# One S5 layer's response matrices: C loaded in another place, evicted in one piece, with the skip added by TensorE

## The chip, the core and the metric

The kernel runs on one core of a Trainium2 chip. The metric is the device time of one execution in microseconds, measured from outside; the profiler's span, from the first to the last instruction, stands beside it. Lower is better.

## The reference, cut to what matters

One inference step of a decoder trunk on 320 tokens (256 of a prompt, 8 samples of 8 tokens). The first layer is an S5 layer: 64 groups of 16 channels, each with 64 complex states, then a GLU. Behind it come a layer with latent attention, and after each of the two an attention to 256 memory tokens and an MLP. Only the S5 layer matters here:

```python
def s5_mixer(u, a_re, a_im, log_dt, b_re, b_im, c_re, c_im, d_skip, w_glu, h0_re, h0_im):
    ...
    _, _, h_re, h_im = lax.associative_scan(
        _complex_affine_combine, (a_seq_re, a_seq_im, bu_re, bu_im), axis=1)
    ...
    y = jnp.einsum('gkn,btgn->btgk', cr, h_re) - jnp.einsum('gkn,btgn->btgk', ci, h_im)
    y = y.reshape(bsz, t, dm) + d_skip.astype(f32) * u.astype(f32)
    g = jax.nn.gelu(y, approximate=False).astype(u.dtype)
    z = g @ w_glu
```

## The kernel before, in words

`s5_scan` computes the layer in chunks of 8 tokens (L = 8; 32 chunks of the prompt and 8 samples make 40 columns). The 64 groups are taken in four quarters `hq` of 16 groups, 8 from each half of the channels. For each quarter three matrices are made from the weights: `rt` turns a chunk's inputs into its state (`state_weights`, `state_turned`, `states`), `ca` turns the state before a chunk into its outputs (`out_weights`), and `tt` holds the responses of a chunk's outputs to its own inputs: a block Toeplitz matrix with 8x8 blocks of 16x16 for each group.

`responses(hq)` (L1097) has TensorE make the 8 blocks of one column, for 16 groups, in one PSUM bank `kps`: four rows of groups q on partitions 32q to 32q+15, four groups j side by side. For quarters 0 and 1, C's part comes in two matrices, `ca` and `ct`, so there are two matmuls for a group; for 2 and 3 one. `responses_out(hq)` (L1110) copies them to `kk` on 16 partitions with four activations (L1114), adds the skip weight D on the diagonal of the first block on GpSimd (`dd` at L1118, `kk` at L1119), and lets SP issue 8 transfers from `kk` to `tt`, one for each input position s (L1122): the first brings 8 blocks to 16 partitions of `tt`, the last one block. `kk` has one buffer, `tt` two. `outputs(hq, half)` (L1168) multiplies the inputs U by `tt` and the states HS by `ca` (and `ct`); its result is evicted (L1193), turned by TensorE and passed through the gelu (`outputs_turned`). `scan(f)` and `scanned(f)` bring the states of quarters 2f and 2f+1 from chunk to chunk; VectorE does the scan.

Between these stand sixteen `products(i)` (L736): matmuls that make the memory layer's keys and values, each of which also issues the weight load of `products(i + 4)` on SP (L219). Their results go out through a pair of buffers by `keys_out` and `values_out`: ScalarE copies, GpSimd issues the transfer (L765). `glu_load(0)` loads the first chunk of the GLU's weights, and `load_gains` nine small rows of gains (L413 to L416), both on SP.

The end of `s5_scan` is a written list of calls, and `in_order` (L600) ties all instructions of `s5_scan` on each engine to the order in which they are written. So an instruction that waits holds up its whole engine, and SP's transfers wait behind each other. Instructions of the GLU that follow can be put between them by the scheduler. SP's transfers take eight semaphores in turn; each waits for the one eight places earlier. `split_chunk` (L185) turns a loaded weight chunk into a high part on ScalarE (L193) and the rest on VectorE (L194) for the GLU's matmuls (L224 to L226).

Of the kernel before, what the change touches and what calls it, by code (L numbers as in the profile page):

```python
# [10 lines left out]
F32 = mybir.dt.float32  # L11
F32R = mybir.dt.float32r
I32 = mybir.dt.int32
AF = mybir.ActivationFunctionType
# [74 lines left out]
class Trunk:  # L89
# [577 lines left out]
    def s5_scan(self, sp, mkv, mn):  # L667
# [50 lines left out]
            PQ.dma_start(xc[i * NCH:i * NCH + NC_P], I['x_prompt'][0].rearrange("(c s) d -> c s d", s=L)[:, :, cols])  # L718
            PQ.dma_start(xc[i * NCH + NC_P:(i + 1) * NCH], I['x_sample'][:, :, cols])
        PQ.tensor_mul(dn, dn, gxn[:G])  # L720
        for i, part in enumerate(('re', 'im')):
            for o in range(2):
                PQ.dma_start(nat['c'][i * G:(i + 1) * G, :, o], I[f'ssm_c_{part}'][0])
        self.mem_load(0, mkv)
        load(0)
        for i, part in enumerate(('re', 'im')):
# [85 lines left out]
        T1 = pp.tile([128, 8, G], F32, name="T1")  # L812
        T2 = pp.tile([128, 8, G], F32, name="T2")
        sign = sp.tile([128, 1], F32, name="sign")
        U = sp.tile([128, G * NCH + 24], F32, name="U")
        tts = [sp.tile([128, L, 16, K], F32, name="tt", tag="tt", bufs=2) for _ in range(2)]
        V.memset(PR[:, 0], 1.0)
        V.memset(PI[:, 0], 0.0)
        V.memset(U[:, G * NCH:], 0.0)
        for hs, v in ((top, 1.0), (bot, -1.0)):  # L820
            V.memset(sign[hs], v)
        for t in tts:
# [45 lines left out]
        def power(m):  # L868
# [15 lines left out]
        cor, coi = w(8), w(9)  # L884
        power(2)

        V.tensor_mul(nat['b'][:, :, 0].rearrange("p k n -> p n k"),
                     bn.rearrange("p (n k) -> p n k", k=K), gxn[:, None, :].to_broadcast([2 * G, N, K]))
        power(4)


# [56 lines left out]
        p4 = lambda ap, gs: ap[:, :, gs].rearrange("p s g -> p g s")[:, :, :, None].to_broadcast([128, 8, L, K])  # L948
        b4 = lambda ap, gs: ap[:, gs, None, :].to_broadcast([128, 8, L, K])
        q4 = lambda ap, gs: ap[:, 1:9, gs].rearrange("p t g -> p g t")[:, :, :, None].to_broadcast([128, 8, L, K])  # L950
        bz = sp.tile([128, 64 * K], F32, name="bz")
        rbs, rts = {}, {}

        def state_weights(hq, hh):

            gs = slice(hh * 32 + 8 * hq, hh * 32 + 8 * hq + 8)
            rb = sp.tile([128, 8, L, K], F32, name="tq", tag="tmp4", bufs=2)
            t1 = sp.tile([128, 8, L, K], F32, name="tq", tag="tq")
            V.tensor_mul(rb, b4(BR, gs), p4(QX, gs))
            V.tensor_mul(t1, b4(BI, gs), p4(QY, gs))  # L960
            V.tensor_add(rb, rb, t1)
            rbs[hq, hh] = rb

        def state_turned(hq, hh):

            if hh == 0:
                rts[hq] = self.xp.tile([128, 2, 8, 128], F32, name="rt", tag="xl" if hq % 2 else "xh", padded_shape=[128, 2, 10, 128])
            rb, rt = rbs.pop((hq, hh)), rts[hq]
            b0 = (hq * 16 + hh * 8) * K
            A.activation(bz[:, b0:b0 + 8 * K].rearrange("p (g k) -> p g k", k=K), rb[:, :, L - 1], AF.Copy)  # L970
            for half in range(2):
                ps = tp("rps")
                for x in range(4):
                    self.transpose(ps[:, x * 128:(x + 1) * 128], rb[:, half * 4 + x].rearrange("p s k -> p (s k)"))
                A.activation(rt[:, hh, half * 4:half * 4 + 4], ps.rearrange("p (x c) -> p x c", x=4), AF.Copy)
# [61 lines left out]
        sc([128, 2, 8, 16])  # L1037
        HW = 32 * NCH
        HSs = [s8.tile([128, HW + 24], F32, name="HS")]
        dd = s8.tile([K, 2, 8, K], F32, name="dd")  # L1040
# [54 lines left out]
        kks = {}  # L1095

        def responses(hq):  # L1097

            ps = kks[hq] = at("kps")
            ca, ct = weights_of(hq)  # L1100
            for j in range(4):
                for q in range(4):
                    u = q * 4 + j
                    o = ps[q * 32:q * 32 + K, j * 128:(j + 1) * 128]
                    z = bz[:, (hq * 16 + u) * K:(hq * 16 + u + 1) * K]
                    nc.tensor.matmul(o, z, ca[u // 8][:, u % 8, 0:L, :], start=True, stop=ct is None, skip_group_check=True)
                    if ct is not None:
                        nc.tensor.matmul(o[:, K:], z, ct[u // 8][:, u % 8, 0:L - 1, :], start=False, stop=True, skip_group_check=True)

        def responses_out(hq):  # L1110
            ps = kks.pop(hq)
            kk = s8.tile([K, L, 16, K], F32, name="kk", tag="kk")
            for q in range(4):
                A.activation(kk[:, :, q * 4:(q + 1) * 4],  # L1114
                             ps[q * 32:q * 32 + K].rearrange("p (j t k) -> p t j k", j=4, t=L), AF.Copy)
            now = kk[:, 0].rearrange("p (h g) k -> p h g k", h=2)
            d = dT.rearrange("p (h g) -> p h g", h=2)[:, :, 8 * hq:8 * hq + 8, None]
            PQ.tensor_mul(dd, d.to_broadcast([K, 2, 8, K]), self.ident[:K, None, None, :K].to_broadcast([K, 2, 8, K]))  # L1118
            PQ.tensor_add(now, now, dd)  # L1119
            tt = tts[hq % 2]  # L1120
            for s in range(L):
                nc.sync.dma_start(tt[s * K:(s + 1) * K, s:], kk[:, 0:L - s])  # L1122


        def scan(f):
# [42 lines left out]
        def outputs(hq, half):  # L1168
            (ca, ct), tt, HS = weights_of(hq), tts[hq % 2], HSs[hq // 2]
            if half == 0:  # L1170
                if hq == 0:
                    ycs[0] = yc0.rearrange("p (s g k) -> p s g k", s=L, k=K)
                elif hq == 2:
                    ygs.append(sp.tile([128, 2, 1024], F32, name="yg", tag="cmat"))
                    ycs[2] = ygs[0][:, 0].rearrange("p (s g k) -> p s g k", s=L, k=K)
                else:
                    pool, tag = (s8, "ct0") if hq == 1 else (sp, "tmp4")
                    ycs[hq] = pool.tile([128, L, 8, K], F32, name="yc", tag=tag, bufs=2)
            ps = at("yps")
            for x in range(4):  # L1180
                gl = half * 4 + x
                n = 2 if ct is None else 3
                for st in range(n):
                    for hh in range(2):
                        g = hh * 32 + hq * 8 + gl
                        g2 = hh * 16 + hq % 2 * 8 + gl
                        o = ps[hh * 64:(hh + 1) * 64, x * 128:(x + 1) * 128]
                        if st == 0:
                            nc.tensor.matmul(o, U[:, g * NCH:g * NCH + 64], tt[:, :, hh * 8 + gl, :], start=True, stop=False)
# [84 lines left out]
        keys_turned(2)  # L1274
        responses(1)
        scanned(0)
        keys_out(2)
        outputs(0, 0)
        responses_out(1)
        outputs(0, 1)  # L1280
        state_weights(2, 0)
        state_turned(2, 0)
        keys_turned(3)
        state_weights(2, 1)
        state_turned(2, 1)
        keys_out(3)
        products(10)
        states(2)
        state_weights(3, 0)
        state_turned(3, 0)  # L1290
        products(11)
        values_out(5)
        state_weights(3, 1)
        state_turned(3, 1)
        states(3)
        outputs(1, 0)
        outputs(1, 1)
        outputs_turned(0)
        outputs_high(0)
        out_weights(2, 0)  # L1300
        out_weights(2, 1)
        products(12)
        responses(2)
        responses_out(2)
        outputs_turned(1)
        outputs_high(1)
        out_weights(3, 0)
        out_weights(3, 1)
        products(13)
        values_out(6)  # L1310
        glu = self.glu_load(0)
        responses(3)
        responses_out(3)
        scan(1)
        products(14)
        products(15)
        gn = self.load_gains(sp)
        scanned(1)
        outputs_low(0)
        outputs_low(1)  # L1320
# [1 line left out]
        outputs(2, 1)  # L1322
        final_states()
        self.chunks_ahead = [self.split_chunk(*glu)]
        values_out(7)
        outputs(3, 0)
        outputs_turned(2)
        outputs_high(2)
        outputs(3, 1)
        outputs_low(2)  # L1330
        outputs_turned(3)
        outputs_high(3)
        outputs_low(3)
# [748 lines left out]
```

## Time and profile before

| | us |
|---|---|
| median of 3 runs | 1212.83 |
| lowest, highest | 1210.83, 1215.29 |
| the profiled execution | 1214.25 |
| its span | 1212.6 |
| TensorE busy (share of the span) | 1130.1 (93%) |
| VectorE busy | 702.0 (58%) |
| ScalarE busy | 552.8 (46%) |
| GpSimd busy | 70.4 (6%) |

The busy times are of the profiled execution, and its own time is 1.42 us above the median of the runs. SP has no row: it computes nothing and only issues transfers. The shares are means over stages, so a stage has to be read by itself: the S5 layer takes about the first 160 us.

### The profile page before, as it was taken

Reading aid. Unit: us, or ns where it says so; the run is one execution under the profiler, and the core shown is the slowest. Engines: PE = TensorE matmul, PEld = TensorE weight load, DVE = VectorE, ACT = ScalarE, POOL = GpSimd, SP = SyncE. Lnnn points to the kernel's source line nnn. Section 1 sums busy time; section 2 is a strip of 40 time slices with the busy share of each in tenths; the row PEclk is TensorE's granted clock in tenths of the full one; section 3 lists DMA queues with packets and bytes.
Section 4 is the critical chain, followed back from the end, with each engine's and each line's share of the span. In section 5 each row is a group of like instructions: output and inputs, shape, how many; then the busy total and the mean of one; then the engine's idle time right before and its main releaser. Section 6 shows DMA issues by size and latency. Waiting matters only on the chain.

```text
span 1212.6 us, 21296 instructions
## 1 busy us (share of the span) xinstructions
PE 1130.1 (93%) x8233; PEld 1023.5 (84%) x8233; DVE 702.0 (58%) x1328; ACT 552.8 (46%) x1009; POOL 70.4 (6%) x118
## 2 busy tenths in 40 slices
PE   4899779899899999999999999999998999999997
PEld 3778669896599999999988985568965899999997
DVE  5898634575359643564587584426852675435643
ACT  3845354444345543453375353224443465434532
POOL 2101100000000000000000054200000000000001
PEclk8999989999899999999999999999999999999999
DMA  9243448746344454545462654547561434545441
GB/s 221 89 119 88 83 145 290 273 139 240 138 122 131 139 161 153 148 149 156 146 183 61 188 180 139 171 139 252 182 224 73 139 100 145 156 143 153 149 147 62
DMA packets 148657, 185.38 MB, mean 153 GB/s; under 512 B 15807, under 2 KB 116428, under 8 KB 148492
## 3 DMA queue, kind: packets, MB, share of 16 engines
q1 hardware_dynamic: 140812, 173.00, 46.6%
q0 software_dynamic: 4000, 7.91, 2.4%
q10 hardware_dynamic: 3744, 3.11, 0.8%
q8 instruction: 65, 1.06, 0.4%
q14 instruction: 36, 0.29, 0.1%
HBM read 175.41 MB, written 6.21 MB: 150 GB/s over the span
## 4 chain that ended last, share of the span: by engine, by line
PE 79%; ACT 7%; DMA 5%; issue 4%; DVE 2%; SPq 2%; POOL 0%; POOLq 0%; ACTq 0%; DVEq 0%
PE mm L224 19%; PE mm L225 19%; PE mm L226 19%; PE kt L102 2%; ACT whi L193 2%; PE sps L1458 2%; PE s L1941 2%; DMA wraw<-in_w_mem_q 2%; PE mm L750 1%; DMA wraw<-in_w_mem_k 1%; DMA wraw<-in_w_glu 1%; PE ops L1473 1%; PE pov L1515 1%; PE s L1982 1%; SPq L1122 1%
## 5 line engine op out<-in xcount | busy, mean ns | idle before, releaser
L194 DVE TENSOR_TENSOR wlo<-wraw,whi 128x1024 fp32r<-128x1024 f32 (+1 forms) x216 | 259.6, 1205 | 295.8 <-ACT whi L193 276.5
L193 ACT ACTIVATE whi<-wraw 128x1024 fp32r<-128x1024 f32 (+1 forms) x216 | 224.4, 1044 | 314.3 <-PE mm L225 249.1
L225 PE MATMUL mm<-xl,whi 128*128 128x320 f32 x944 | 294.4, 314 | 0.8 <-DVE xl L1704 0.6
L224 PE MATMUL mm<-xh,whi 128*128 128x320 f32 x944 | 281.5, 317 | 8.9 <-ACT xh L1485 4.5
L226 PE MATMUL mm<-xh,wlo 128*128 128x320 f32 x944 | 282.5, 312 | 0.0
L224 PEld LDWEIGHTS mm<-xh,whi 128*128 128x128 f32 x944 | 176.1, 191 | 11.8 <-ACT xh L1485 5.0
L225 PEld LDWEIGHTS mm<-xl,whi 128*128 128x128 f32 x944 | 180.6, 191 | 2.3 <-DVE xl L301 0.8
L226 PEld LDWEIGHTS mm<-xh,wlo 128*128 128x128 f32 x944 | 177.5, 191 | 0.0
L224 PE MATMUL mm<-hh,whi 128*128 128x320 f32 x512 | 158.0, 309 | 0.0
L225 PE MATMUL mm<-hl,whi 128*128 128x320 f32 x512 | 158.0, 309 | 0.0
L226 PE MATMUL mm<-hh,wlo 128*128 128x320 f32 x512 | 157.1, 308 | 0.0
L225 PEld LDWEIGHTS mm<-hl,whi 128*128 128x128 f32 x512 | 96.1, 188 | 0.0
L224 PEld LDWEIGHTS mm<-hh,whi 128*128 128x128 f32 x512 | 96.1, 188 | 0.0
L226 PEld LDWEIGHTS mm<-hh,wlo 128*128 128x128 f32 x512 | 95.9, 188 | 0.0
L102 PE MATMUL kt<-ident,kn 128*128 128x128 f32 x256 | 38.4, 285 | 7.3 <-ACT ktb L1385 4.2
L102 PEld LDWEIGHTS kt<-ident,kn 128*128 128x128 f32 x256 | 28.3, 143 | 19.5 <-ACT ktb L1385 6.8
L1870 POOL DMA_DIRECT2D rop<-in_cache_k_rope x64 | 34.4, 537 | 39.2 <-issue 16.6
L118 DVE TENSOR_TENSOR sq<-sq 128x320 f32<-128x320 f32 x67 | 32.3, 482 | 2.4 <-ACT sq L120 1.6
L1574 DVE TENSOR_TENSOR t_up<-t_up 128x320 f32<-128x320 f32 x64 | 29.8, 486 | 1.9 <-ACT hh L1573 1.8
L1575 DVE TENSOR_TENSOR hl<-t_up,hh 128x320 fp32r<-128x320 f32 x64 | 29.8, 487 | 0.9
L1383 DVE COPY ktb<-kt 128x512 f32<-128x512 f32 x32 | 22.0, 688 | 12.4 <-PE kt L102 11.9
L1573 ACT ACTIVATE hh<-t_up 128x320 fp32r<-128x320 f32 x64 | 28.4, 472 | 0.9
(493 smaller groups left out, 1805.1 us busy)
## 6 DMA issues: line engine op xcount, KB each, us to landing
wraw<-in_w_mlp_up SPq DMA_DIRECT2D x64, 512.0 KB, 3.7
wraw<-in_w_mlp_down SPq DMA_DIRECT2D x64, 512.0 KB, 3.5
kn<-in_cache_mem_k SPq DMA_DIRECT2D x16, 1024.0 KB, 7.1
vn<-in_cache_mem_v SPq DMA_DIRECT2D x16, 1024.0 KB, 9.7
wraw<-in_w_glu SPq DMA_DIRECT2D x32, 256.0 KB, 3.9
wraw<-in_w_mem_q SPq DMA_DIRECT2D x16, 512.0 KB, 6.8
wraw<-in_w_mem_o SPq DMA_DIRECT2D x16, 512.0 KB, 3.8
lat<-in_cache_kv_latent SPq DMA_DIRECT2D x64, 128.0 KB, 2.6
```

The costliest lines, as they stand in the source:

```text
L102: return self.nc.tensor.transpose(out, in_, self.ident[b:b + k, b:b + k])
L118: eng.tensor_add(st['acc'], st['acc'], st['last'])
L193: nc.scalar.activation(hi[:, :cols], raw[:, :cols], AF.Copy)
L194: nc.vector.tensor_sub(lo[:, :cols], raw[:, :cols], hi[:, :cols].bitcast(F32))
L224: nc.tensor.matmul(ps, wh, xh, start=start, stop=False)
L225: nc.tensor.matmul(ps, wh, xl, start=False, stop=False)
L226: nc.tensor.matmul(ps, wl, xh, start=False, stop=stop)
L1458: nc.tensor.matmul(sps[h * 32:(h + 1) * 32, :MT], qm[:, h * 2 + db, j * 128 + i * 32:j * 128 + (i + 1) * 32], ktb[:, h * 2 + db, :], start ...
L1573: A.activation(hh[b // 4][:, b % 4, :], a, AF.Square)
L1574: V.tensor_mul(a, a, a)
L1575: V.tensor_sub(hl[b // 4][:, b % 4, :], a, hh[b // 4][:, b % 4, :].bitcast(F32))
L1870: last[eng] = eng.dma_start(dst, src[bass.ds(v, 1)].rearrange("o p d -> (o p) d"))
```

## The change

It does four things. The four transfers of C are written further down, in a block that is to be issued after the VectorE operation `gained`. `responses` lets TensorE add the skip weights, by one more matmul of the identity with `dd` for each group, and makes its tiles 32 partitions high (16 of them from a neighbour's columns of `bz`, never read), so that all 128 partitions of the bank are written. `responses_out` evicts the bank with one activation into `kk` with 128 partitions and two halves, and issues four transfers for each s, one for each q. And in the list of calls `keys_out(2)`, `keys_out(3)`, `values_out(5)` and `values_out(7)` stand later, `products(12)` to `(14)`, `glu_load(0)` and `load_gains` earlier.

```diff
@@ s5_scan, loads @@
-        for i, part in enumerate(('re', 'im')):
-            for o in range(2):
-                PQ.dma_start(nat['c'][i * G:(i + 1) * G, :, o], I[f'ssm_c_{part}'][0])
...
+        gained = V.tensor_mul(nat['b'][:, :, 0].rearrange("p k n -> p n k"),
+                              bn.rearrange("p (n k) -> p n k", k=K), gxn[:, None, :].to_broadcast([2 * G, N, K]))
+        with tc.issue_after(gained.ins):
+            for i, part in enumerate(('re', 'im')):
+                for o in range(2):
+                    PQ.dma_start(nat['c'][i * G:(i + 1) * G, :, o], I[f'ssm_c_{part}'][0])
@@ responses @@
+            d = dT.rearrange("p (h g) -> p h g", h=2)[:, :, 8 * hq:8 * hq + 8, None]
+            PQ.tensor_mul(dd.rearrange("p (h g) k -> p h g k", h=2), d.to_broadcast([K, 2, 8, K]),
+                          self.ident[:K, None, None, :K].to_broadcast([K, 2, 8, K]))
...
-                    o = ps[q * 32:q * 32 + K, j * 128:(j + 1) * 128]
-                    z = bz[:, (hq * 16 + u) * K:(hq * 16 + u + 1) * K]
-                    nc.tensor.matmul(o, z, ca[u // 8][:, u % 8, 0:L, :], start=True, stop=ct is None, skip_group_check=True)
+                    o = ps[q * 32:(q + 1) * 32, j * 128:(j + 1) * 128]
+                    z = bz[:, hq, u * K:(u + 2) * K]
+                    nc.tensor.matmul(o, z, ca[u // 8][:, u % 8, 0:L, :], start=True, stop=False, skip_group_check=True)
...
+                    nc.tensor.matmul(o[:, :K], self.ident[:K, :2 * K], dd[:, u, :], start=False, stop=True, skip_group_check=True)
@@ responses_out @@
-            kk = s8.tile([K, L, 16, K], F32, name="kk", tag="kk")
-            for q in range(4):
-                A.activation(kk[:, :, q * 4:(q + 1) * 4],
-                             ps[q * 32:q * 32 + K].rearrange("p (j t k) -> p t j k", j=4, t=L), AF.Copy)
-            now = kk[:, 0].rearrange("p (h g) k -> p h g k", h=2)
...
-            PQ.tensor_add(now, now, dd)
+                kk_of.append(s8.tile([128, 2, L, 4, K], F32, name="kk", tag="kk", padded_shape=[128, 4, L, 4, K]))
+            kk = kk_of[0][:, hq % 2]
+            A.activation(kk, kks.pop(hq).rearrange("p (j t k) -> p t j k", j=4, t=L), AF.Copy)
             tt = tts[hq % 2]
             for s in range(L):
-                nc.sync.dma_start(tt[s * K:(s + 1) * K, s:], kk[:, 0:L - s])
+                for q in range(4):
+                    nc.sync.dma_start(tt[s * K:(s + 1) * K, q, s:], kk[q * 32:q * 32 + K, 0:L - s])
@@ the list of calls @@
         scanned(0)
-        keys_out(2)
         outputs(0, 0)
...
         state_turned(2, 0)
+        keys_out(2)
         keys_turned(3)
...
-        keys_out(3)
         products(10)
         states(2)
+        keys_out(3)
...
         states(3)
+        values_out(5)
+        products(12)
+        glu = self.glu_load(0)
         outputs(1, 0)
...
-        products(12)
+        products(13)
         responses(2)
...
-        products(13)
         values_out(6)
-        glu = self.glu_load(0)
+        products(14)
+        gn = self.load_gains(sp)
         responses(3)
         responses_out(3)
         scan(1)
-        products(14)
         products(15)
-        gn = self.load_gains(sp)
         scanned(1)
...
-        values_out(7)
         outputs(3, 0)
...
         outputs_low(2)
+        values_out(7)
         outputs_turned(3)
```

How this moves instructions is seen on three queues. First SP, from the responses of the last quarter to the GLU's weights; `tt<-kk` are the responses' transfers, `gn` the gains, `wraw` weights. Before:

```order
L1122 DMA tt<-kk 16x2048
L1122 DMA tt<-kk 16x1792
L1122 DMA tt<-kk 16x1536
L1122 DMA tt<-kk 16x1280
L1122 DMA tt<-kk 16x1024
L1122 DMA tt<-kk 16x768
L1122 DMA tt<-kk 16x512
L1122 DMA tt<-kk 16x256
L413 DMA gn<-in_norm_mix_pre 16x128
```

The same place after the change:

```order
L416 DMA gn<-in_q_norm 3x128
L1125 DMA tt<-kk 16x512 x4
L1125 DMA tt<-kk 16x448 x4
L1125 DMA tt<-kk 16x384 x4
L1125 DMA tt<-kk 16x320 x4
L1125 DMA tt<-kk 16x256 x4
L1125 DMA tt<-kk 16x192 x4
L1125 DMA tt<-kk 16x128 x4
L1125 DMA tt<-kk 16x64 x4
L182 DMA wraw<-in_w_glu 128x2x256 x6
```

Eight transfers became 32 with the same bytes, the gains stand ahead of them, and the first GLU weights but one chunk stay behind them. The other three quarters changed in the same way.

Second, ScalarE's queue from the states HS to the fourth quarter's outputs `yc`; `yg` are those of the third, `whi` the splits of GLU weights. Before:

```order
L1163 ACTIVATE HS<-H 64x16x32
L1193 ACTIVATE yg<-yps 128x8x64
L193 ACTIVATE whi<-wraw 128x1024
L1193 ACTIVATE yg<-yps 128x8x64
L193 ACTIVATE whi<-wraw 128x1024
L790 ACTIVATE wlo<-mm,r_mem 128x256 x2
```

And after:

```order
L1166 ACTIVATE HS<-H 64x16x32
L1196 ACTIVATE yg<-yps 128x8x64 x2
L193 ACTIVATE whi<-wraw 128x1024 x2
L1196 ACTIVATE yc<-yps 128x8x64
L1212 ACTIVATE yg<-ytp 128x80x4 x2
L193 ACTIVATE whi<-wraw 128x1024
```

The first split no longer stands between the two evictions of `yg`, and the last `values_out` (`wlo<-mm`) is gone from this place. Third, GpSimd's queue at the start, with its waits; `natc` is C, `dn` and `hn` are D and the states that come in. Before:

```order
L720 TENSOR_TENSOR dn<-dn,gxn 64x16 [waits DMASW2_49,DMASW0_49]
L723 DMA natc<-in_ssm_c_re 64x16x64
L723 DMA natc<-in_ssm_c_re 64x16x64 [waits DMASW1_49]
L723 DMA natc<-in_ssm_c_im 64x16x64
L723 DMA natc<-in_ssm_c_im 64x16x64 [waits DMASW3_49]
```

And after:

```order
L720 TENSOR_TENSOR dn<-dn,gxn 64x16 [waits DMASW2_49,DMASW0_49]
L891 DMA natc<-in_ssm_c_re 64x16x64
L891 DMA natc<-in_ssm_c_re 64x16x64 [waits DMASW1_49]
L891 DMA natc<-in_ssm_c_im 64x16x64
L891 DMA natc<-in_ssm_c_im 64x16x64 [waits DMASW3_49]
```

Only the line numbers differ; no wait on VectorE has come in.

## Rows read from the trace of the kernel before

**Rows 1.** The page: the span in 40 slices, TensorE's busy tenths and GB/s moved.

```profile
PE   4899779899899999999999999999998999999997
...
GB/s 221 89 119 88 83 145 290 273 139 240 138 122 131 139 161 153 148 149 156 146 183 61 188 180 139 171 139 252 182 224 73 139 100 145 156 143 153 149 147 62
```

**Rows 2.** SP's queue in order of time: start us, us, engine line op out<-in xcount.

```profile
75.88 7.26 SPq L1122 DMA_DIRECT2D tt<-kk  x8
...
138.76 5.96 SPq L1122 DMA_DIRECT2D tt<-kk  x8
```

**Rows 3.** The chain that ended last, where it runs through SP: start us, us, what.

```profile
138.76 0.51 SPq L1122
139.31 0.59 SPq L1122
139.95 0.59 SPq L1122
...
144.13 0.59 SPq L1122
...
145.24 0.35 SPq L413
...
148.45 0.23 SPq L415
...
149.08 0.39 SPq L182
```

**Rows 4.** ScalarE in order of time, with idle time before a row and its releaser.

```profile
72.61 2.40 ACT L1114 ACTIVATE kk<-kps 16x512 f32<-16x512 f32 x4 [2.03 <-PE kps L1108]
...
92.56 0.60 ACT L1193 ACTIVATE wlo<-yps 128x512 f32<-128x512 f32 x1
...
135.28 2.39 ACT L1114 ACTIVATE kk<-kps 16x512 f32<-16x512 f32 x4 [6.07 <-DMA tt<-kk]
...
154.74 1.06 ACT L193 ACTIVATE whi<-wraw 128x1024 fp32r<-128x1024 f32 x1 [11.27 <-DMA wraw<-in_w_glu]
```

**Rows 5.** TensorE in order of time, 59 to 163 us.

```profile
59.32 2.06 PE L1058 MATMUL sps<-U,rt 128*64 128x40 f32 x64
...
85.68 0.44 PE L1189 MATMUL yps<-tt,U 128*64 128x128 f32 x4
...
93.21 0.44 PE L1189 MATMUL yps<-tt,U 128*64 128x128 f32 x4 [3.20 <-ACT wlo L1193]
...
95.98 1.09 PE L102 MATMUL rps<-ident,tq 128*128 128x128 f32 x8
...
111.62 0.30 PE L1189 MATMUL yps<-tt,U 128*64 128x128 f32 x1
...
117.09 1.09 PE L102 MATMUL ytp<-ident,wlo 128*128 128x128 f32 x8
118.02 3.62 PE L752 MATMUL mm<-wraw,mnp 128*128 128x256 f32 x16
121.57 1.46 PE L1106 MATMUL kps<-hca,bz 128*16 128x128 f32 x32
122.96 1.09 PE L102 MATMUL ytp<-ident,yc 128*128 128x128 f32 x8
...
156.33 1.97 PE L102 MATMUL ytp<-ident,yg 128*128 128x128 f32 x8 [7.61 <-ACT yg L1193]
158.23 0.70 PE L1189 MATMUL yps<-tt,U 128*64 128x128 f32 x4
...
162.46 0.39 PE L224 MATMUL mm<-xh,whi 128*128 128x320 f32 x1
```

**Rows 6.** The transfers of line L1122: time from issue to landing.

```profile
DMA to landing us min/median/max: 2.2/4.0/5.1
```

**Rows 7.** Busy time in a stretch: engines, then granted TensorE clock, DMA share, GB/s.

```profile
156.00:158.00 2.00, 1.67 (x8) 1.57 (x8) 0.74 (x1) 2.00 (x5) 0.00 (x0) 0.50 0.00 0
```

**Rows 8.** The DMA view, 138 to 148 us: queue, packets, MB, share of 16 engines.

```profile
q1 hardware_dynamic: 382, 0.62, 55.3%
```

**Rows 9.** GpSimd in order of time.

```profile
6.28 1.67 POOL L723 DMA_DIRECT2D natc<-in_ssm_c_re  x2
```

More of the change, by code (lines that the diff above doesn't have):

```diff
@@ L814, in s5_scan @@
         sign = sp.tile([128, 1], F32, name="sign")
+        bz = sp.tile([128, 4, 17 * K], F32, name="bz")
         U = sp.tile([128, G * NCH + 24], F32, name="U")
-        tts = [sp.tile([128, L, 16, K], F32, name="tt", tag="tt", bufs=2) for _ in range(2)]
+        tts = [sp.tile([128, 4, L, 4, K], F32, name="tt", tag="tt", bufs=2) for _ in range(2)]
         V.memset(PR[:, 0], 1.0)
@@ L819, in s5_scan @@
         V.memset(U[:, G * NCH:], 0.0)
+        V.memset(bz[:, :, 16 * K:], 0.0)
         for hs, v in ((top, 1.0), (bot, -1.0)):
@@ L885, in s5_scan @@
         power(2)
-        V.tensor_mul(nat['b'][:, :, 0].rearrange("p k n -> p n k"),
-                     bn.rearrange("p (n k) -> p n k", k=K), gxn[:, None, :].to_broadcast([2 * G, N, K]))
+        gained = V.tensor_mul(nat['b'][:, :, 0].rearrange("p k n -> p n k"),
[4 more added lines that the diff above has]
+                    PQ.dma_start(nat['c'][i * G:(i + 1) * G, :, o], I[f'ssm_c_{part}'][0])
         power(4)
@@ L950, in s5_scan @@
         q4 = lambda ap, gs: ap[:, 1:9, gs].rearrange("p t g -> p g t")[:, :, :, None].to_broadcast([128, 8, L, K])
-        bz = sp.tile([128, 64 * K], F32, name="bz")
         rbs, rts = {}, {}
@@ L968, in state_turned @@
             rb, rt = rbs.pop((hq, hh)), rts[hq]
-            b0 = (hq * 16 + hh * 8) * K
-            A.activation(bz[:, b0:b0 + 8 * K].rearrange("p (g k) -> p g k", k=K), rb[:, :, L - 1], AF.Copy)
+            b0 = hh * 8 * K
+            A.activation(bz[:, hq, b0:b0 + 8 * K].rearrange("p (g k) -> p g k", k=K), rb[:, :, L - 1], AF.Copy)
             for half in range(2):
@@ L1039, in s5_scan @@
         HSs = [s8.tile([128, HW + 24], F32, name="HS")]
-        dd = s8.tile([K, 2, 8, K], F32, name="dd")
+        dd = s8.tile([K, 16, K], F32, name="dd")
         ca_of = lambda q: [s8.tile([128, 8, 9, K], F32, name="ca", tag=f"ca{q}", bufs=2) for _ in range(2)]
@@ L1093, in weights_of @@
             return ca, cts.get(hq)
-        kks = {}
+        kks, kk_of = {}, []
         def responses(hq):
+            d = dT.rearrange("p (h g) -> p h g", h=2)[:, :, 8 * hq:8 * hq + 8, None]
+            PQ.tensor_mul(dd.rearrange("p (h g) k -> p h g k", h=2), d.to_broadcast([K, 2, 8, K]),
+                          self.ident[:K, None, None, :K].to_broadcast([K, 2, 8, K]))
             ps = kks[hq] = at("kps")
@@ L1103, in responses @@
                     u = q * 4 + j
-                    o = ps[q * 32:q * 32 + K, j * 128:(j + 1) * 128]
-                    z = bz[:, (hq * 16 + u) * K:(hq * 16 + u + 1) * K]
-                    nc.tensor.matmul(o, z, ca[u // 8][:, u % 8, 0:L, :], start=True, stop=ct is None, skip_group_check=True)
+                    o = ps[q * 32:(q + 1) * 32, j * 128:(j + 1) * 128]
+                    z = bz[:, hq, u * K:(u + 2) * K]
+                    nc.tensor.matmul(o, z, ca[u // 8][:, u % 8, 0:L, :], start=True, stop=False, skip_group_check=True)
                     if ct is not None:
-                        nc.tensor.matmul(o[:, K:], z, ct[u // 8][:, u % 8, 0:L - 1, :], start=False, stop=True, skip_group_check=True)
+                        nc.tensor.matmul(o[:, K:], z, ct[u // 8][:, u % 8, 0:L - 1, :], start=False, stop=False, skip_group_check=True)
+                    nc.tensor.matmul(o[:, :K], self.ident[:K, :2 * K], dd[:, u, :], start=False, stop=True, skip_group_check=True)
         def responses_out(hq):
-            ps = kks.pop(hq)
-            kk = s8.tile([K, L, 16, K], F32, name="kk", tag="kk")
-            for q in range(4):
-                A.activation(kk[:, :, q * 4:(q + 1) * 4],
-                             ps[q * 32:q * 32 + K].rearrange("p (j t k) -> p t j k", j=4, t=L), AF.Copy)
-            now = kk[:, 0].rearrange("p (h g) k -> p h g k", h=2)
-            d = dT.rearrange("p (h g) -> p h g", h=2)[:, :, 8 * hq:8 * hq + 8, None]
-            PQ.tensor_mul(dd, d.to_broadcast([K, 2, 8, K]), self.ident[:K, None, None, :K].to_broadcast([K, 2, 8, K]))
-            PQ.tensor_add(now, now, dd)
+            if not kk_of:
+                kk_of.append(s8.tile([128, 2, L, 4, K], F32, name="kk", tag="kk", padded_shape=[128, 4, L, 4, K]))
+            kk = kk_of[0][:, hq % 2]
+            A.activation(kk, kks.pop(hq).rearrange("p (j t k) -> p t j k", j=4, t=L), AF.Copy)
             tt = tts[hq % 2]
             for s in range(L):
-                nc.sync.dma_start(tt[s * K:(s + 1) * K, s:], kk[:, 0:L - s])
+                for q in range(4):
+                    nc.sync.dma_start(tt[s * K:(s + 1) * K, q, s:], kk[q * 32:q * 32 + K, 0:L - s])
         def scan(f):
@@ L1188, in outputs @@
                         if st == 0:
-                            nc.tensor.matmul(o, U[:, g * NCH:g * NCH + 64], tt[:, :, hh * 8 + gl, :], start=True, stop=False)
+                            nc.tensor.matmul(o, U[:, g * NCH:g * NCH + 64], tt[:, (hh * 8 + gl) // 4, :, gl % 4, :], start=True, stop=False)
                         else:
@@ L1291, in s5_scan @@
         products(11)
-        values_out(5)
         state_weights(3, 1)
```

## The prediction

> **What bounds the kernel now.** Read the page's slices first [rows 1]. Each slice is 30.3 us. From the ninth on TensorE is busy nine tenths or more nearly everywhere, so there a later start is passed on whole. The slack lies in the first eight, where the S5 layer stands, and everything the change touches lies between 60 and 163 us. Then read the SP queue [rows 2]: `responses_out` issues eight transfers `tt<-kk` for each of four quarters, in 7.26 us the first time and 5.96 us the last. Then the chain of waits, which gives them one by one [rows 3], and last the two engines that wait on them, ScalarE [rows 4] and TensorE [rows 5]. Three stalls are plain in ScalarE's rows: the eviction into `kk` waits 6.07 us for the transfers before it, since there is one `kk`; and a weight split waits 11.27 us for a GLU weight that SP could issue only after the last responses and the gains. TensorE's first GLU matmul starts at 162.46 us. That instant is what I follow: the change is worth what it moves it by.
>
> **What the change takes away.** Four evictions of 16 partitions (2.40 us) become one on 128 partitions; the nearest row of that shape is 0.60 us [rows 4]. The GpSimd addition behind it goes off the path. `kk` gets two halves, so the 6.07 us wait goes; the split is now queued behind both evictions of `outputs(2)`, so the 11.27 us no longer stand before the second of them. I count all of these at nothing except the first: a later `tt` covers them, as the next parts show.
>
> **What it adds on TensorE.** 16 matmuls of 32x16 for each quarter, 32 records. The nearest small ones are `sps`, 64 records in 2.06 us [rows 5], so 32 take at most 1.0 us; the 32 records of `responses(2)` take 1.4 us with eight times the columns, which is no lower. I take 0.9 us, four times; nothing to 1.0 us are the ends.
>
> **What it adds on SP.** This decides. Each burst of 8 becomes 32 issues, with the same bytes. A large piece is slowed by the transfers ahead of it, but the unhindered issues of a burst show a price that hardly hangs on size: 0.59 us for 112 KB (the one at 139.31), 0.59 for 96 KB, 0.59 for 16 KB (the last), and 0.64 us from start to start [rows 3]. The new pieces are 32 KB to 4 KB. From other tensors come cheaper ones: the nine gain loads from HBM take 145.24 to 149.08, 0.43 us each, and the least, with two rows, 0.23 us. So the bounds are 0.43 and 0.65 us; I take 0.63, since the same tensors at nearly the same size show it. A burst then holds SP for 32 x 0.63 = 20.2 us, and its last piece lands 31 x 0.63 + 2.2 = 21.7 us after the first issue, with the least landing time [rows 6].
>
> **The sum, instant by instant.** `responses(0)` ends about when `kk` starts, 72.61 us. Plus 0.9 for the matmuls and 0.7 for the eviction and its hand-over, SP starts at 74.2 (75.88 before) [rows 2]. `tt` is whole at 74.2 + 21.7 = 95.9. TensorE, in order, stands at `outputs(0, 0)`, which started at 85.68. A half of `outputs(0)` takes 2.7 us (93.21 to 95.98, by the starts of it and the next work), and an eviction with hand-over 0.7 stands between: 95.9 + 2.7 + 0.7 + 2.7 = 102.0 against 95.98, so **6.0 us lost**; the 3.2 us that TensorE waited before that second half, which the later `keys_out(2)` removes, lie inside.
>
> Nothing shortens the run of TensorE to 111.62, so `outputs(1, 0)` would come at 117.6, and at 121.2 with `products(12)` moved ahead of it (3.55 us, 118.02 to 121.57). The second burst starts when `outputs(0, 0)` and `kk` are evicted, 98.6 + 1.4 = 100.0; SP, free of the first burst at 94.4 and of three weight loads behind it (0.5 each) at 96, is ready. Its `tt` is whole at 121.7, a half microsecond late. From there `outputs(1)` 5.5 us (111.62 to 117.09), the turn 0.9, `products(13)` 3.55, `responses(2)` 1.4 + 0.9, eviction 0.7: SP starts the third burst at 134.6.
>
> Now SP itself is the path. Third burst 20.2, to 154.8; then the nine gain loads, which the change moves ahead of the fourth burst, 3.84, to 158.6 [rows 3]; the fourth burst's `tt` is whole at 158.6 + 21.7 = 180.3. Its `kk` is ready long before, since `responses(3)` follows `responses(2)` within 7 us, and the scan, moved by the same 6.0 us, too. `outputs(3, 0)` waits for the transfers. TensorE has by then idled twice for over 10 us; after its idle time before 156 us the granted clock was 0.50 for two microseconds, so 1.2 GHz [rows 7], and the eight turns took 1.97 us where they take 1.09 at the full clock [rows 5]. So `outputs(3, 0)`, 16 matmuls where the 2.7 us held 24, takes 3.6 us, up to 3.9 with its start, the turn 1.9, and from `outputs(3, 1)` to the first GLU matmul it is 162.46 - 158.23 = 4.2: 180.3 + 3.9 + 1.9 + 4.2 = 190.3. That is **27.9 us later** than 162.46. Six GLU weight loads stand right behind the fourth burst (178.8), so they land by then. What comes after has the same order; the last `values_out` now stands after `outputs(3)` and the second weight split needs its buffer, which can cost some 3 us more, and prefetch can give that back.
>
> The profiled execution took 1214.25 us (span 1212.6), 1.4 above the median of the three runs, so 1214.25 + 27.9 - 1.4 = **1241 us**.
>
> Loading C later I count at nothing. The wait that the block adds holds only for instructions on VectorE, where `gained` runs; the transfers are GpSimd's, and the order shows them in the same place with no wait on VectorE.
>
> **The rivals.** *Cheap issues.* If a piece costs what a gain load does, 0.43 us, a burst holds SP for 13.8 us and `tt` is whole after 15.5. Then `outputs(0)` ends at 95.8, no loss; the third burst starts at 128.1, the gains end at 145.7, the last `tt` is whole at 161.2 and GLU starts at 171.2: 8.7 late, 1221.5 us. For it: all these are rows with 16 or fewer partitions from the same queue. Against it: the shortest of the 32 `tt` issues takes 0.51 us, the first of its burst, on an idle queue [rows 3].
>
> *Issues hidden behind transfers, so faster.* SP's rows may show long issues only because the transfers ahead of them are slow, and 32 small ones may pass as fast as their bytes allow. The window of the last burst has the hardware queue at 55.3% of 10 us, 5.5 us for 0.62 MB [rows 8]. With bursts of 6 us the third starts at 128, the gains end at 138, the last `tt` is whole at 146.3 and GLU starts at 153.5, now at the full clock, because none of the removed waits is replaced: 9 us early, 1204 us. It decides at about 0.33 us for a piece: with 7.2 us from the last `tt` to GLU, 162.46 - 128.1 - 3.84 - 2.2 - 7.2 = 21.1 us are left for 63 issues. Against it: the last piece of each burst, 16 KB, still takes 0.59 us with nothing ahead that it must wait for, and only transfers of two or three rows are under 0.33 [rows 3]. The Trainium skill, "DMA: Bandwidth & Descriptors", section "Issuing engines are not separate DMA queues", holds that the time on the sequencer to start a DMA is usually small relative to the DMA itself. By that rule the bursts would end as in this rival, at 1204 us; the row at 144.13 speaks against it, since 16 KB, a thirty-sixth of the burst's bytes, cost a tenth of the burst's issue time.
>
> *C does move.* Then 1.05 MB leave the start, where the first weights are waited for; at the 290 GB/s of the seventh slice [rows 1] that is 3.6 us at most, and the sum is 1237 to 1241. Against it: their place on their queue, where they start at 6.28 us now [rows 9], is the same in both orders.
>
> **How the numbers follow.** Forecast, issues of 0.55 to 0.70 us: 0.75, at 1233 to 1250 us with the 3 us behind GLU's start. Cheap issues, 0.35 to 0.55: 0.19, at 1217 to 1233. Hidden issues: 0.03. C moves, with the forecast's issues: 0.03. I take 1241. The range reaches down to the price of the gain loads and up to 0.70 us with the late split: 1221 to 1250. A measurement can tell about 0.5%, 6 us, from no change. Slower by more: all of the forecast and most of the cheap issues, 0.93; within: their lowest part, 0.04; faster: the hidden issues, 0.03.
>
> **What would show it.** In the profile after: 128 `tt<-kk` issues of about 0.58 us, bursts of some 20 us in SP's rows; TensorE idle before `outputs(0, 0)` until about 96, before `outputs(2, 0)` until about 156 and before `outputs(3, 0)` until about 180; the first GLU matmul near 190; the GpSimd rows of `natc` still at 6 to 9 us; no wait of `kk` on `tt`. It is wrong if the pieces take under 0.5 us, if `outputs(3, 0)` starts before 170 us, or if GLU starts late and the end does not.

## The result, and the profile after

The change makes the kernel slower, and by more than my range allowed. Five runs of each, side by side:

| | before | after |
|---|---|---|
| median, us | 1214.05 | 1264.46 |
| lowest, highest | 1210.83, 1216.19 | 1256.38, 1266.69 |
| ratio (95% interval) | | 1.0387 (1.0346 to 1.0428) |
| profiled execution, span | 1214.25, 1212.6 | 1256.38, 1254.7 |

I forecast 1241 us, between 1221 and 1250. The profiled execution of the changed kernel is the lowest of its five, 8.1 us under their median; the trace therefore accounts for 42.1 us of the 50.4 between the medians, and the rest stays without a row.

The slices of the page show idle time of TensorE where it was expected. Compare with [rows 1]:

```profile
PE   4999966999989999999998999999999999999997
```

Slices six and seven, 157 to 220 us, now hold idle TensorE; from the eighth on nothing has changed in kind. Slices three to five read busy and hide the rest of the loss, as the rows below show. SP's queue in order of time has the long bursts of the forecast, beside [rows 2]:

```profile
83.31 20.73 SPq L1125 DMA_DIRECT2D tt<-kk  x32
...
111.11 21.94 SPq L1125 DMA_DIRECT2D tt<-kk  x32
...
152.44 20.11 SPq L1125 DMA_DIRECT2D tt<-kk  x32
172.64 0.52 SPq L413 DMA_DIRECT2D gn<-in_norm_mix_pre  x1
...
174.60 1.57 SPq L413 DMA_DIRECT2D gn<-in_norm_mlp_pre  x1
...
177.72 20.13 SPq L1125 DMA_DIRECT2D tt<-kk  x32
```

The view of the tile `tt` gives the price of one piece, with its least, median and longest time in ns, and the time to landing, which answers to [rows 6]:

```profile
L1125 SPq DMA_DIRECT2D tt<-kk x128: 512/587/1609, 83.3 to 197.3; - x128
...
DMA to landing us min/median/max: 1.7/1.9/3.6
```

So far the forecast holds: 0.587 us for a piece, 20.1 to 21.9 us for a burst. But the first burst starts at 83.31 us where I had 74.2. ScalarE's rows, beside [rows 4], say what it waited for:

```profile
82.68 0.60 ACT L1121 ACTIVATE kk<-kps 128x512 f32<-128x512 f32 x1 [11.18 <-PE kps L1115]
...
151.81 0.60 ACT L1121 ACTIVATE kk<-kps 128x512 f32<-128x512 f32 x1 [7.69 <-PE kps L1115]
```

The eviction is one row of 0.60 us, as hoped, and no `kk` waits for `tt` any more; it waits 11.18 us for TensorE's matmuls of line L1115, the skip. TensorE in order of time, with idle time before a row in brackets, beside [rows 5]:

```profile
71.58 0.41 PE L1111 MATMUL kps<-ca,bz 128*32 128x128 f32 x2
71.82 0.36 PE L1113 MATMUL kps<-ct,bz 128*32 128x112 f32 x2
72.10 0.23 PE L1115 MATMUL kps<-dd,ident 16*32 16x16 f32 x2
72.27 0.41 PE L1111 MATMUL kps<-ca,bz 128*32 128x128 f32 x2
...
94.01 0.41 PE L1111 MATMUL kps<-ca,bz 128*32 128x128 f32 x2
...
96.63 0.23 PE L1115 MATMUL kps<-dd,ident 16*32 16x16 f32 x2 [2.03 <-POOL dd L1102]
...
107.11 0.44 PE L1192 MATMUL yps<-tt,U 128*64 128x128 f32 x4
...
133.94 0.29 PE L1192 MATMUL yps<-tt,U 128*64 128x128 f32 x1 [0.59 <-DMA tt<-kk]
...
143.77 0.41 PE L1111 MATMUL kps<-hca,bz 128*32 128x128 f32 x2
...
151.71 1.09 PE L102 MATMUL ytp<-ident,yc 128*128 128x128 f32 x8
...
197.21 0.66 PE L1192 MATMUL yps<-tt,U 128*64 128x128 f32 x2 [20.29 <-DMA tt<-kk]
198.43 0.47 PE L1192 MATMUL yps<-tt,U 128*64 128x128 f32 x1 [0.56 <-DMA tt<-kk]
...
202.83 0.44 PE L1192 MATMUL yps<-tt,U 128*64 128x128 f32 x4
...
207.68 1.40 PE L102 MATMUL ytp<-ident,yc 128*128 128x128 f32 x8 [2.89 <-ACT yc L1196]
...
208.95 0.62 PE L224 MATMUL mm<-xh,whi 128*128 128x320 f32 x1
```

From one group to the next it is 72.27 - 71.58 = 0.69 us, sixteen groups 11.0 us. In the kernel before the same stretch reads:

```profile
70.66 0.43 PE L1106 MATMUL kps<-ca,bz 128*16 128x128 f32 x8
...
71.08 0.42 PE L1106 MATMUL kps<-ca,bz 128*16 128x128 f32 x8
...
72.45 3.72 PE L750 MATMUL mm<-mnp,whi 128*128 128x256 f32 x16
```

Each matmul leaves two records, so x8 are four groups, one in each strip of 32 columns of the array, and they start together: four groups in 71.08 - 70.66 = 0.42 us, all sixteen in 72.45 - 70.66 = 1.8 us. In the changed kernel every row is one matmul (x2), and each starts 0.17 to 0.28 us after the one before. The idle bracket does not show this: the engine counts as busy, at the full granted clock (1.00 in the stretch from 71.5 to 82.6 us), while one strip works at a time.

GpSimd, beside [rows 9]: C starts where it did, and the diagonal blocks `dd` of the second quarter now stand on the path, behind two output transfers:

```profile
6.27 1.67 POOL L891 DMA_DIRECT2D natc<-in_ssm_c_re  x2
...
94.51 1.44 POOL L762 DMA_DIRECT2D out<-wlo  x2 [5.88 <-ACT wlo L787]
95.97 0.61 POOL L1102 TENSOR_TENSOR dd<-dT,ident 16x256 f32<-16x256 f32 x1
```

### The profile page after: what moved, and what is told of

It is laid out like the page before. It is cut to its first block, busy times and chain, and to the rows that moved or that the text cites. A ratio compares the mean times of both kernels' runs of the same rounds, so it can differ in the third digit from the quotient of the medians.

```text
span 1254.7 us, 21614 instructions
## 1 busy us (share of the span) xinstructions
PE 1163.6 (93%) x8361; PEld 1043.3 (83%) x8361; DVE 700.3 (56%) x1329; ACT 545.9 (44%) x997; POOL 68.1 (5%) x114
## 4 chain that ended last, share of the span: by engine, by line
PE 76%; SPq 5%; ACT 5%; issue 5%; DMA 4%; DVE 3%; POOL 0%; POOLq 0%; ACTq 0%; DVEq 0%
PE mm L225 18%; PE mm L224 18%; PE mm L226 18%; SPq L1125 4%; PE kt L102 2%; PE sps L1461 2%; PE s L1944 2%; DMA whi<-in_w_mem_k 2%; ACT whi L193 1%; DMA wraw<-in_w_glu 1%; PE ops L1476 1%; PE pov L1518 1%; PE s L1985 1%; DMA wraw<-in_w_mem_q 1%; PE ltp L102 1%
## 5 line engine op out<-in xcount | busy, mean ns | idle before, releaser
L1192 PE MATMUL yps<-tt,U 128*64 128x128 f32 x128 | 16.9, 295 | 22.1 <-DMA tt<-kk 21.4
L1192 PEld LDWEIGHTS yps<-tt,U 128*64 128x64 f32 x128 | 11.6, 148 | 24.1 <-issue 22.1
```

The costliest lines, as they stand in the source:

```text
L1192: nc.tensor.matmul(o, U[:, g * NCH:g * NCH + 64], tt[:, (hh * 8 + gl) // 4, :, gl % 4, :], start=True, stop=False)
```

## The experiments

| kernel | median, us | ratio (95% interval) | first GLU matmul, us |
|---|---|---|---|
| changed, skip behind | 1246.25 | 1.0238 (1.0198 to 1.0278) | 196.6 |
| changed, skip of 128 rows | 1243.58 | 1.0221 (1.0196 to 1.0247) | 194.4 |
| before, wide strips | 1216.05 | 1.0001 (0.9986 to 1.0016) | 168.0 |
| before, skip by TensorE alone | 1240.39 | 1.0195 (1.0170 to 1.0220) | 189.4 |
| before, list of the change | 1213.14 | 0.9981 (0.9965 to 0.9998) | 162.3 |
| before, list and mended skip | 1215.68 | 1.0004 (0.9985 to 1.0023) | 166.7 |
| before, C late in fact | 1212.12 | 0.9973 (0.9951 to 0.9994) | 163.9 |
| skip of 128 rows, two queues | 1219.20 | 1.0033 (1.0017 to 1.0048) | 170.4 |
| before, list and C late | 1209.02 | 0.9948 (0.9930 to 0.9965) | 162.1 |
| the same, splits held | 1202.51 | 0.9906 (0.9875 to 0.9938) | 151.0 |
| the change mended | 1212.10 | 0.9970 (0.9951 to 0.9989) | 157.1 |

Each ratio is to runs of the kernel before on the same chip (1214.9 to 1215.9 us); the last column is of each profiled execution, and between executions the S5 stage as a whole lies up to 4 us earlier or later. Two of the profiled executions lie apart from their medians: 1226.21 us with the wide strips, 1196.07 us with the splits held.

**The skip matmuls behind the others.** In `responses`, the changed kernel:

```diff
-                    nc.tensor.matmul(o[:, :K], self.ident[:K, :2 * K], dd[:, u, :], start=False, stop=True, ...)
+            for j in range(4):
+                for q in range(4):
+                    u = q * 4 + j
+                    o = ps[q * 32:(q + 1) * 32, j * 128:(j + 1) * 128]
+                    nc.tensor.matmul(o[:, :K], self.ident[:K, :2 * K], dd[:, u, :], start=False, stop=True, ...)
```

Issued behind the others, the skip isn't added to every group's sum, so this run is read for the time of its instructions, which are all there.

> The changed kernel with one edit: the sixteen skip matmuls of a quarter stand behind all its other matmuls instead of one behind each group. The trace of the changed kernel has the matmuls of the first quarter from 71.58 to 82.58 us, 11.0 us, 0.69 us for each group; before the change four groups, one in each strip of 32 columns, started within 40 ns of each other. Theory: the skip matmul, with 16 rows between matmuls of 128 rows, lets the groups no longer run side by side. Then this kernel needs 1.7 us as before plus 0.2 to 1.0 us for sixteen small ones, at most 2.7 us for a quarter; the rest of my first sum holds, the long bursts of SP decide, and the first GLU matmul starts near 190 us (208.95 in the changed kernel, 162.46 before): 19 us less, so about 1238 to 1246 us. The Trainium skill, page TensorEngine Tiling (Array Packing), section Key Properties, states that a change of the tiling mode drains the engine; with that rule this is the outcome. Rival: strips 32 columns wide, or a third matmul in a group, end the concurrency by themselves; then a quarter still takes some 8 to 11 us and the time stays near 1264.

TensorE's rows of the first quarter:

```profile
72.87 0.45 PE L1111 MATMUL kps<-ca,bz 128*32 128x128 f32 x8
73.11 0.39 PE L1113 MATMUL kps<-ct,bz 128*32 128x112 f32 x8
...
74.72 0.44 PE L1119 MATMUL kps<-dd,ident 16*32 16x16 f32 x32
75.09 0.70 PE L747 MATMUL mm<-mnp,whi 128*128 128x256 f32 x2
```

The x8 are back, all sixteen skip matmuls take 0.4 us, and the quarter 2.2 us instead of 11.0. The time came out at the upper end of what was expected, the first GLU matmul at 196.6 us where about 190 was. The same sixteen matmuls cost 0.4 us or 9 us, by where they stand.

**The skip matmul over 128 rows, in its old place.**

```diff
-        dd = s8.tile([K, 16, K], F32, name="dd")
+        ddz = s8.tile([128, 16, K], F32, name="dd")
+        PQ.memset(ddz, 0.0)
+        dd = ddz[:K]
-                    nc.tensor.matmul(o[:, :K], self.ident[:K, :2 * K], dd[:, u, :], start=False, stop=True, ...)
+                    nc.tensor.matmul(o[:, :K], self.ident[:, :2 * K], ddz[:, u, :], start=False, stop=True, ...)
```

> The changed kernel with the skip matmul left in its place, but over 128 rows: the diagonal blocks lie in a tile of 128 partitions, of which 112 are zero, and the identity is taken with 128 rows. So every matmul of a quarter has the same shape of 128 rows by 32 columns. Theory (a change of rows stops the side by side): the groups run side by side again, a quarter takes 1.7 us plus at most 1.0 us, and the time is that of the kernel with the skip behind, 1238 to 1246 us. Rival (a third matmul with another stationary operand in each group, or the width): a quarter takes 8 us or more as in the changed kernel and the time stays near 1264 us.

TensorE's rows of the first quarter, with three matmuls a group, and of the third, with two:

```profile
69.77 0.41 PE L1113 MATMUL kps<-ca,bz 128*32 128x128 f32 x2
70.02 0.26 PE L1115 MATMUL kps<-ct,bz 128*32 128x112 f32 x1
70.02 0.30 PE L1113 MATMUL kps<-ca,bz 128*32 128x128 f32 x1
...
74.07 0.92 PE L747 MATMUL mm<-mnp,whi 128*128 128x256 f32 x3
...
134.64 0.42 PE L1113 MATMUL kps<-hca,bz 128*32 128x128 f32 x4
134.88 0.23 PE L1117 MATMUL kps<-dd,ident 128*32 128x16 f32 x4
135.04 0.45 PE L1113 MATMUL kps<-hca,bz 128*32 128x128 f32 x8
```

Another matmul with another operand doesn't by itself put the groups in single file: with 128 rows throughout, neighbours overlap again, and the time is 21 us under the change. With two matmuls a group four run abreast (x8); with three only neighbours overlap, 74.07 - 69.77 = 4.3 us a quarter where I allowed 2.7. So a part of the rival holds: a third matmul in a group does cost, 2.5 us a quarter beside the 9.2 of the change, and why was not tried.

**Strips of 32 columns alone.** In the kernel before, `o = ps[q * 32:(q + 1) * 32, ...]` and `z` two groups wide.

> The kernel before with one edit: the tiles of responses are 32 columns wide instead of 16 (bz is set to zero once). Theory: nothing but the height of the tiles differs, four groups still run side by side, a quarter with two matmuls a group takes 1.7 us as before, and the time is that of the kernel before, 1210 to 1217 us. Rival (a full strip of 32 columns ends the concurrency): a quarter takes sixteen times 0.4 to 0.5 us, 6 to 8 us, and the time is 1225 to 1240 us.

```profile
73.92 0.45 PE L1107 MATMUL kps<-ca,bz 128*32 128x128 f32 x8
```

Still x8, and the ratio is 1.0001 (0.9986 to 1.0016). The width is free.

**The skip by TensorE alone, on the kernel before.**

```diff
+                    nc.tensor.matmul(o[:, :K], self.ident[:K, :K], dd[:, u, :], start=False, stop=True, ...)
...
-            PQ.tensor_add(now, now, dd)
```

> The kernel before with only the skip weights added by TensorE, one small matmul behind each group, without the addition on GpSimd; eviction, eight transfers a quarter and the order of the calls are those of before. Theory: the quarters take 11.0 us instead of 1.7 (0.69 us for each group, as in the changed kernel) for the first two and 7.9 instead of 1.2 to 1.4 for the other two. The first two delay TensorE by some 17 to 20 us before outputs(1, 0), the third by 6.5 us and the fourth is partly hidden; the first GLU matmul starts between 183 and 194 us and the time is 1234 to 1246 us. By my first sum, which took 0.9 us for a quarter, it would be within 4 us of the kernel before.

```profile
70.55 0.39 PE L1109 MATMUL kps<-ca,bz 128*16 128x128 f32 x2
70.78 0.35 PE L1111 MATMUL kps<-ct,bz 128*16 128x112 f32 x2
71.06 0.21 PE L1112 MATMUL kps<-dd,ident 16*16 16x16 f32 x2
71.20 0.39 PE L1109 MATMUL kps<-ca,bz 128*16 128x128 f32 x2
```

0.65 us a group, and 25 us in all, with bursts of 5.8 to 6.9 us. So the loss has two halves of like size: 1.0195 for the skip, 1.0221 for the pieces and the rest with the skip mended; their product, 1.042, lies within the interval of the whole, 1.0346 to 1.0428.

**Two queues.** The kernel with the skip of 128 rows, pieces with q of 2 and 3 issued by GpSimd: `(nc.sync if q < 2 else PQ).dma_start(...)`.

> The kernel with skip matmuls of 128 rows (1243.6 us, GLU from 194.4 us, bursts of 21 us), with half of the 32 pieces of each quarter issued by GpSimd instead of SP. Theory: what decides there is the number of pieces that one queue issues. SP's half takes 10.2 us; GpSimd's sixteen at 0.75 to 0.84 us, as its other transfers show, take 12 to 13.4 us beside it. The third and fourth bursts shrink by 8 us each, and the first two by less than they delayed: the first GLU matmul starts 16 to 22 us earlier, and the time is 1221 to 1229 us. Rival: the pieces are slow because of what they move, 16 partitions each, and not because of their issues; then two queues bring little, and the time stays within 4 us of 1243.6.

```profile
L1127 SPq DMA_DIRECT2D tt<-kk x64: 512/588/1330, 76.4 to 160.3; - x64
L1127 POOL DMA_DIRECT2D tt<-kk x64: 487/487/563, 76.6 to 154.1; - x64
```

The time falls by 24 us to 1219.2, a little more than expected; GpSimd needs 0.487 us for a piece where I had 0.75 to 0.84. The pieces and their bytes are the same as before, so what the bursts cost is the number of pieces on one queue.

**The list of calls alone.**

> The kernel before with the list of calls of the changed kernel and nothing else: evictions, eight transfers a quarter and GpSimd's addition are those of before. Theory: the order is not what made the change slow. TensorE no longer waits 3.2 us for the second half of outputs(0), nothing new is added, and the bursts stay at 6 to 7 us; the gains, now ahead of the fourth burst, take back 3.8 us of it. The first GLU matmul starts between 157 and 163 us, and the time is 1207 to 1216 us. Rival: the order itself brings waits (a later values_out, gains ahead of the burst), and the time is 1220 us or more.

The order is no loss; it gains 0.2%, barely clear of the noise (0.9965 to 0.9998). ScalarE's rows show what is left behind the bursts:

```profile
152.53 1.06 ACT L193 ACTIVATE whi<-wraw 128x1024 fp32r<-128x1024 f32 x1 [11.10 <-DMA wraw<-in_w_glu]
```

**The list and the mended skip with eight transfers.** The skip has 128 rows, `dd` is made one quarter ahead, and `load_gains` stands behind the fourth `responses_out`.

> The kernel before with the parts of the change that should pay: the list of calls of the changed kernel, but with the gains behind the fourth burst, and the skip weights added by TensorE with matmuls of 128 rows, whose diagonal blocks GpSimd makes one quarter ahead. The four evictions on 16 partitions and the eight transfers a quarter stay. Theory: responses take 2 to 4 us a quarter, GpSimd's addition and the 3.2 us stall of TensorE are gone, no burst is longer than 7 us. The sum of my rival with short bursts put the first GLU matmul at 153.5 us, 9 us earlier than before; with the evictions of 2.4 us in place it is 154 to 159, and the time 1204 to 1211 us. If the parts of the change bring nothing even with short bursts, it is 1212 us or more.

A miss: 1215.68 us. No matmul of the responses waits for `dd`, but the gains push the GLU's chunks back on SP, and the same split of ScalarE waits longer:

```profile
156.02 1.06 ACT L193 ACTIVATE whi<-wraw 128x1024 fp32r<-128x1024 f32 x1 [12.72 <-DMA wraw<-in_w_glu]
```

I had freed everything ahead of that wait and not the wait. The next runs aim at it.

**C late in fact**, on the kernel before: the four transfers behind `V.memset(nat['c'][:, 0, :, 0:1], 0.0)`, which stands behind the gains on B, so that they must wait.

> The kernel before with C loaded later in fact: VectorE writes one column of C's tile behind the gains on B, and the four transfers, written behind it, must wait for that. In the changed kernel they start at 6.3 us as before. My third rival gave this at most 3.6 us: then the time is 1209 to 1215 us. The other side: C lands some 15 us after its start and the turning matmuls use it from 40 us on, so if the gains on B come after 25 us the stage starts later by what is missing, and the loads of the states behind C on GpSimd's queue come later too; the time is then up to 1235 us.

```profile
23.51 1.68 POOL L889 DMA_DIRECT2D natc<-in_ssm_c_re  x2 [17.14 <-DVE natc L886]
```

They start at 23.5 us, land in 5.0 to 7.1 us (13.0 to 17.1 before), and the time is 0.27% lower. What the change says of C would have paid a little; the block it uses doesn't do it.

**Both, and then the splits held.** The second adds a hold on ScalarE's splits of the GLU's second to fourth chunk:

```diff
+        self.hold = {i: self.s5_high for i in range(101, 104)}
```

`s5_high` is the last activation of `outputs_high(3)`.

> The two parts that measured faster than before by themselves, together: the list of calls of the changed kernel (ratio 0.9981) and C loaded behind the gains on B (0.9973), on the kernel before, nothing else. If they act in different stretches they add: 0.9954, some 1208 to 1212 us. Rival: ScalarE's split of a GLU chunk, which waits until that chunk lands at 152.4 us with the evictions of outputs(2) queued behind it, sets the end in both, so the second adds nothing: 1211 to 1215 us.

> The kernel with both, and with ScalarE's splits of the GLU's second to fourth chunk held behind the last outputs, so that no eviction of outputs waits 11.1 us for a chunk. Theory: this wait is what stands behind the short bursts in every version; without it outputs(3, 0) follows the last tt at about 148 us and the first GLU matmul comes near 153 to 157 us, 5 to 9 us earlier. If that passes on, 1201 to 1207 us. Rival: the GLU then waits for its own chunks, which land no earlier, and gives all or most of it back: 1207 to 1213 us.

The first two add, 0.9948. With the splits held, ScalarE and TensorE read:

```profile
143.21 0.60 ACT L1194 ACTIVATE yg<-yps 128x512 f32<-128x512 f32 x1 [1.64 <-PE yps L1193]
143.83 1.06 ACT L193 ACTIVATE whi<-wraw 128x1024 fp32r<-128x1024 f32 x1
```

```profile
144.48 0.44 PE L1190 MATMUL yps<-tt,U 128*64 128x128 f32 x4 [1.31 <-DMA tt<-kk]
...
151.03 0.39 PE L224 MATMUL mm<-xh,whi 128*128 128x320 f32 x1
```

The 11 us wait is gone, and at 1202.5 us this kernel is faster than the one before, 0.9906 (0.9875 to 0.9938), and than the one without the hold. Its six runs spread from 1196.07 to 1208.37 us, and the rows are of the fastest.

**The change mended**: skip of 128 rows, `dd` a quarter ahead, two queues, gains behind, C late, splits held.

> The changed kernel's own design with what the runs found mended: skip matmuls of 128 rows, the diagonal blocks made a quarter ahead, half the pieces issued by GpSimd, the gains behind the fourth burst, C late in fact, and the splits held. Against the kernel with two queues (1219.2 us) the second quarter no longer waits 2.6 us and the fourth 5.6 us for GpSimd's diagonal blocks, and the fourth burst starts up to 5 us earlier. Theory: eviction in one piece pays no more than it costs in pieces; 1205 to 1213 us, no faster than the kernel with the splits held. Rival: one piece does pay once the bursts are shared, and this one is the fastest by over 3 us.

1212.1 us, as expected: slightly better than before and 10 us behind the kernel that keeps four evictions and eight transfers. TensorE shows where it loses:

```profile
148.39 0.68 PE L1201 MATMUL yps<-tt,U 128*64 128x128 f32 x3 [6.86 <-DMA tt<-kk]
```

`outputs(3, 0)` waits for the fourth `tt` until 148.39 us, in the kernel above until 144.48, since SP issues its 32 pieces of the last two quarters one behind the other in 21.7 us. After that wait the granted clock is 0.50 from 148.3 to 152.2 us. So eviction in one piece, with its 32 transfers, does not pay here. It isn't shown that all of the 10 us are its price: this kernel also keeps the skip on TensorE, 4.3 us for each of the first two quarters.

## Why the prediction was wrong

**The step that failed** is the one under "What it adds on TensorE": "16 matmuls of 32x16 for each quarter ... I take 0.9 us, four times; nothing to 1.0 us are the ends." I priced them by other small matmuls, the 64 records of `sps` in 2.06 us [rows 5]. As work they are cheaper still, 0.4 us when they stand behind. But in their place they stop the other matmuls of the quarter from running four abreast: the first two quarters took 11.0 us each where I had 2.7 (1.8 and the 0.9), and the third 7.9 where I had 2.3. That this is the rows of the operand, 16 among 128, is shown by four runs: alone, on the kernel before, they cost 25 us; behind the others they take 0.4 us a quarter; with 128 rows, most of the loss is gone; the width of the strips changes nothing. The Trainium skill, page "TensorEngine Tiling (Array Packing)", section "Key Properties", states that changing the tiling mode drains the engine. The traces agree with it, at about 0.6 us for each group of two changes (0.69 against 0.42 / 4 = 0.10), though the drain itself has no row. It was the rule against this change, and I didn't weigh it.

Instant by instant, in us:

| | predicted | measured |
|---|---|---|
| SP starts the first burst | 74.2 | 83.31 |
| `outputs(0, 0)` starts | 95.9 | 107.11 |
| `outputs(1, 0)` runs on | 121.7 | 133.94 |
| SP starts the third burst | 134.6 | 152.44 |
| the gains end | 158.6 | 177.7 |
| the first GLU matmul | 190.3 | 208.95 |

The first two quarters of matmuls made TensorE itself the path to `outputs(0, 0)`: 94.01 to 107.1 us for the second quarter, 2.03 of it the wait for `dd`, so the first burst was covered, and `outputs(1, 0)` ran on 12.2 us later than forecast. The third quarter added 5.6. These are the 17.8 us at the third burst. From there to the GLU I had 55.7 us and it took 56.5, and that is in part luck. The gains took 5.1 us where I had 3.84, and the last `tt` came 20.7 us behind them for 21.7. `outputs(3, 0)` and the turn took 202.83 - 198.43 = 4.4 us where I had 5.8. The last stretch took 208.95 - 202.83 = 6.1 us where I had 4.2: 2.89 of it is a wait for `yc`, whose eviction stands on ScalarE behind the late weight split, the some 3 us that I had named and kept out of the sum:

```profile
205.37 1.06 ACT L193 ACTIVATE whi<-wraw 128x1024 fp32r<-128x1024 f32 x1 [1.15 <-DMA wraw<-in_w_glu]
```

**What held.** A piece costs 0.587 us and 0.63 from start to start, at whatever size; the bursts of the last two quarters are 20.1 us; the eviction is 0.60 us; `kk` waits for no transfer; C doesn't move, and its rival fell. Both other rivals fell with the 0.43 and 0.33 us they needed: 32 issues took three times the 6 to 7 us in which eight carried the same bytes. The Trainium skill, page "DMA: Bandwidth & Descriptors", section "Issuing engines are not separate DMA queues", calls the time to start a transfer usually small relative to the transfer. This trace doesn't agree: it was 0.587 us of the queue for each piece, beside 1.9 us to landing, and it set the path. With the skip at 128 rows, which cost 2.5 us in the first quarter and 0.3 in the third where I had 0.9, the forecast's own numbers nearly appear: GLU at 194.4 us for 190.3, and 1243.6 us for 1241. The idle spells I named came out in part: 20.29 us before `outputs(3, 0)`, but none before `outputs(0, 0)` and `outputs(2, 0)`, where the long matmuls stood.

**What I left out besides.** `dd` moved from behind the responses to their front, on a queue with output transfers ahead of it: 2.03 and 1.35 us of TensorE's time, where I had called GpSimd's part off the path. Of the three stalls that I counted in ScalarE's rows I named two; no third enters the sum. And a later GLU start is not passed on whole: 46.5 us there are 42.1 in the span, 32.0 are 29.3 with the skip of 128 rows; I had passed it on whole. In the kernel before the GLU waits 2.19 us for a chunk at 173.03 us; the changed kernel shows no such wait up to 225 us. That is half of the 4.4 us; the rest stays open.

## What to carry to other kernels

A small matmul is priced by what it does to its neighbours: read in the trace whether the rows around it start together in several strips, and give it the same number of rows, or, where the sums allow it, a place behind them (here they don't). A transfer that is cut in four costs four issues on its queue; where the issues are the path, bytes and landing times say nothing. And before paying for an earlier start, find the wait that stands behind it: the 11 us wait of a split on ScalarE held two sound improvements to 0.5% together until it was moved.

## What was not expected of the hardware

An engine that reads busy at the full granted clock did the work of 1.8 us in 11.0. In the fourth quarter, where TensorE was off the path, it read busy for all of 160 to 168 us, again one matmul at a time, at a mean granted clock of 0.53; why it fell was not tried. GpSimd issued the small transfers faster than SP, 0.487 against 0.587 us, sixteen of them in 7.75 us, though I had priced it by its output transfers and those of C, 0.72 to 0.84; its small loads at the start, 0.52 to 0.62, were the nearer rows. And matmuls in one kind of strip, three to a group, overlapped only by pairs (4.3 us a quarter) where two to a group ran four abreast; this stays open.
